# Gate products in blocks of 1024 columns with seven-product quads, placed first, then delta groups, v, u and z

## The chip, the cores and the metric

The kernel runs on one core of a Trainium2 chip. The metric is the device time of one launch in microseconds. The matrix engine is called PE here, the vector engine DVE, the scalar engine ACT, GpSimd POOL, and SP is the queue that issues the loads and stores.

## The reference

One layer, 256 positions, width 4096, all in float32:

```python
def reference(x, norm_g, w_in, ...):
    h = rms_norm(x, norm_g[l])
    proj = h @ w_in[l]                                  # 4096 x 22560
    u_pre, v_pre, z_gm, qkv_pre, z_dn, b_pre, a_pre, gate_gm, gate_dn = split_columns(proj)
    y_gm = gmlp_spatial_gating(gelu(u_pre), gelu(v_pre), ln_g[l], ln_b[l], w_s[l], b_s[l])
    y_gm = (y_gm * silu(z_gm)) @ w_br_gmlp[l]           # 2048 x 4096
    qkv = silu(causal_depthwise_conv(qkv_pre, conv_w[l]))
    q, k, v = ...                                       # 16 heads of 128, q and k normalised
    o = gated_delta_rule(q, k, v, beta, g)              # chunks of 64, a triangular solve in each
    y_dn = (rms_norm(o, dn_norm_g[l]) * silu(z_dn)) @ w_br_dn[l]
    merged = sigmoid(gate_gm) * y_gm + sigmoid(gate_dn) * y_dn
    return rms_norm(x + merged @ w_out[l], final_g)
```

The two gates take 8192 of the columns of w_in.

## The kernel before

A float32 product is made of three fast ones: each operand is split into a rounded part h and a rest l, and xh·h + xh·l + xl·h is summed in PSUM (`mms`, lines 170 to 179; L177 is xh·h, L178 xh·l, L179 xl·h). The sequence's two halves of 128 positions are m = 0 and 1; the split of x stays in SBUF as `xs` (eight tiles, h and l of four row tiles each).

A **job** is 512 columns of a weight matrix: all row tiles (32 of 128 rows for `w_in` and `w_out`, 16 for the two `w_br`), two at a time (`KPD`). A unit of two row tiles is one load of 512 KB (`raw`, five buffers, `fetch`), one cast on ACT (`wh`, L166), one subtraction on DVE (`wl`, L167) and 12 products of 128x512 on PE into two PSUM banks (`acc`, six buffers in pool `pm`; two more banks, `side`, serve all else through `bank()`). `wh` and `wl` have four buffers each. `stream` (L181 on) walks over all units in the order of the list `jobs` and writes the split of a unit three units ahead of its products (`LEAD`).

The order of jobs (L905 on): four v, then u and z by turns (four each), then four delta groups of v, k, q and z_dn (`done_conv`, `done_zd`), each followed by three gate jobs (`done_gate`; the last group by seven), then 16 half jobs of `w_br`, then 8 of `w_out`. After a job its `done` puts a generator in lane 0, which evicts the banks and does the elementwise work; lane 1 holds the longer chains: the delta rule of a group, `dn_gen`, which begins when q's conv is done, and at the end the loads of `ys`. `step` advances both lanes once per unit, a `yield n` waits n units, and `drain` runs them empty (before the pools are closed and opened anew: `open_a`, `open_c`, `open_d`). A scheduler then orders the instructions of each engine; engines work in that order.

A conv (L479 to L534) evicts a job to `vtok`, `ktok` or `tok`, stores it, loads it back shifted by 1 to 3 rows (`tok4`, four buffers) and multiplies and adds on DVE (L501, L503, L504); k and q are turned by a transpose on DVE and 24 corner copies, 12 per half, on ACT (`turn`, L126 to L135). The solve in `dn_gen` is 31 pairs of small operations on DVE (L613, L615).

Of the kernel before, what the change touches and what calls it, by code (L numbers as in the profile page):

```python
# [31 lines left out]
WARM = 9  # L32


class Job:
    def __init__(self, w, col, nk, src, done, before=None):
        self.w, self.col, self.nk, self.src = w, col, nk, src
        self.done, self.before = done, before


@with_exitstack
def trunk(ctx, tc, t):
# [10 lines left out]
    def bank():  # L53
        return ps.tile([P, 512], F32, name="side")
# [125 lines left out]

    def stream():  # L181
        units = [(j, k) for j in jobs for k in range(0, j.nk, KPD)]
        raws, sp, acc, late = {}, {}, None, []
        for i in range(len(units) + LEAD):
            if i == 0:
                for n in range(4):
                    raws[n] = fetch(*units[n], n == 0)
                    first_x(n)
            elif i + 3 < len(units):
                first_x(i + 3)  # L190
                raws[i + 3] = fetch(*units[i + 3])
            if i < len(units):
                if i == 0:
                    sp[i] = split0(raws.pop(i))
                else:
                    split_x(i)
                    sp[i] = split(raws.pop(i), i >= len(units) - TAIL)
            n = i - LEAD
            if n >= 0:
                j, k = units[n]  # L200
                if k == 0:
                    if j.before:
                        j.before()
# [45 lines left out]
    lng = pb.tile([P, W], F32, name="lng")  # L249
    lnb = pb.tile([P, W], F32, name="lnb")  # L250
    wst = pb.tile([P, 16, P], F32, name="wst")
    bs = pb.tile([P, 16], F32, name="bs")
    vg = [pb.tile([P, W], F32, name=f"vg{m}") for m in range(2)]
    vsum = pb.tile([P, 8], F32, name="vsum")
    st = pb.tile([P, 16], F32, name="st")

    def norm_gen():
        yield 12
        xend = xs[KT // 4 - 1][:, 1, 3, S - 1:S].bitcast(F32)
        for m in range(2):  # L260
            for c in range(8):
                xt = pb.tile([P, NC], F32, name="xt", bufs=3)
# [12 lines left out]
    def const_gen():  # L275
        yield 36
        zz = pb.tile([3, NC], F32, name="zz")
        after([lng[:, 0:1], lnb[:, 0:1], wst[:, 0, 0:1], bs[:, 0:1], dng[:, 0:1], alog[:, 0:1], dtb[:, 0:1],
               ident[:, 0:1], upr[:, 0:1], low[:, 0:1], zz[:, 0:1]], rstd[:, 1:2])
        nc.sync.dma_start(out=ident, in_=t["ident"])  # L280
        nc.sync.dma_start(out=lng, in_=t["ln_g"].partition_broadcast(P))
        yield 2
        nc.sync.dma_start(out=lnb, in_=t["ln_b"].partition_broadcast(P))
        yield 2
        nc.sync.dma_start(out=wst, in_=t["w_sT"])
        yield 2
        G.memset(wst[64:P, :, 0:64], 0.0)
        nc.sync.dma_start(out=bs, in_=t["b_sT"])
# [702 lines left out]
```

## Time and profile before

| | |
|---|---|
| median of three runs | 2736.73 us (2734.74 to 2739.87) |
| the profiled execution | 2738.57 us |
| its span | 2736.8 us |
| PE busy | 2708.8 us, 99% |
| DVE busy | 1613.9 us, 59% |
| ACT busy | 1379.4 us, 50% |
| granted clock of PE | 0.998 of full |

The span goes from the first to the last instruction. Busy time is the union of an engine's instructions; a product is 389 ns long in the records but the next starts 0.23 us later, so counts per stretch tell PE's rate better than busy time does.

### The profile page before, as it was taken

What the parts mean: (1) busy time and instruction counts of PE and PEld (TensorE: products, weight loads), DVE (VectorE), ACT (ScalarE), POOL (GpSimd) and SP (SyncE); (2) the same over time, 40 slices, a digit from 0 to 9 for tenths busy, and PEclk for the clock granted to TensorE, in tenths of its full rate; (3) what the DMA queues carried; (4) which work ended last, traced back from release to release, by engine and by line L of the source; (5) the groups of instructions that cost most, each with busy time, mean ns of one, the idle gap of its engine ahead of it and who ended that gap; (6) DMA issues with size and microseconds to landing.
All of it is one profiled execution on the core that took longest, in us unless ns stands there. A gap on an engine that the chain in (4) does not pass through costs nothing.

```text
span 2736.8 us, 33340 instructions
## 1 busy us (share of the span) xinstructions
PE 2708.8 (99%) x12385; PEld 2235.7 (82%) x12385; DVE 1613.9 (59%) x2092; ACT 1379.4 (50%) x1917; POOL 38.2 (1%) x44
## 2 busy tenths in 40 slices
PE   9999999999999999999999999999999999999998
PEld 7888888888788877888788887888878888888886
DVE  6464555466665676746757576564556656645544
ACT  7544555455544455445554456444545655644443
POOL 0000000000000000000000000000000000000000
PEclk9999999999999999999999999999999999999999
DMA  9866676677777676767767676776776666576665
GB/s 327 264 182 202 200 195 197 182 241 241 232 208 200 216 261 202 216 192 232 256 200 211 212 236 218 206 216 177 230 257 210 224 209 223 178 244 217 207 216 170
DMA packets 325292, 595.57 MB, mean 218 GB/s; under 512 B 33636, under 2 KB 47972, under 8 KB 324744
## 3 DMA queue, kind: packets, MB, share of 16 engines
q1 hardware_dynamic: 324840, 593.28, 70.8%
q8 instruction: 97, 1.59, 0.2%
q14 instruction: 67, 0.55, 0.1%
q10 hardware_dynamic: 288, 0.15, 0.0%
HBM read 569.16 MB, written 24.19 MB: 217 GB/s over the span
## 4 chain that ended last, share of the span: by engine, by line
PE 85%; DMA 4%; DVE 4%; ACT 3%; issue 2%; POOL 1%; SPq 0%; DVEq 0%; POOLq 0%
PE acc L177 28%; PE acc L178 28%; PE acc L179 27%; DVE wl L167 1%; DMA cw<-conv_w 1%; ACT wh L166 1%; DMA preq<-tok 1%; ACT kT L135 1%; DVE tok L503 1%; DMA yr<-yds 1%; DMA prek<-ktok 1%; DMA raw<-w_in 0%; DMA yr<-ygs 0%; DMA tok<-prek 0%; POOL rq L97 0%
## 5 line engine op out<-in xcount | busy, mean ns | idle before, releaser
L167 DVE TENSOR_TENSOR wl<-raw,wh 128x1024 fp32r<-128x1024 f32 x954 | 1160.8, 1223 | 928.6 <-ACT wh L166 920.4
L166 ACT CAST wh<-raw 128x1024 fp32r<-128x1024 f32 x954 | 994.9, 1050 | 1196.7 <-PE acc L179 1119.0
L178 PE MATMUL acc<-wl,xs 128*128 128x512 f32 x3308 | 1291.5, 391 | 8.5 <-DVE wl L167 8.1
L177 PE MATMUL acc<-wh,xs 128*128 128x512 f32 x3308 | 1286.9, 391 | 7.3 <-ACT wh L166 7.0
L179 PE MATMUL acc<-wh,xs 128*128 128x512 f32 x3308 | 1285.8, 390 | 0.0
L178 PEld LDWEIGHTS acc<-wl,xs 128*128 128x128 f32 x3308 | 621.8, 188 | 144.4 <-DVE wl L167 17.6
L177 PEld LDWEIGHTS acc<-wh,xs 128*128 128x128 f32 x3308 | 621.2, 188 | 140.0 <-ACT wh L166 10.5
L179 PEld LDWEIGHTS acc<-wh,xs 128*128 128x128 f32 x3308 | 621.4, 188 | 128.6
L179 PE MATMUL acc<-wh,ys 128*128 128x512 f32 x512 | 199.2, 389 | 0.0
L178 PE MATMUL acc<-wl,ys 128*128 128x512 f32 x512 | 199.2, 389 | 0.0
L177 PE MATMUL acc<-wh,ys 128*128 128x512 f32 x512 | 195.8, 389 | 0.0
L179 PEld LDWEIGHTS acc<-wh,ys 128*128 128x128 f32 x512 | 96.1, 188 | 20.1
L178 PEld LDWEIGHTS acc<-wl,ys 128*128 128x128 f32 x512 | 96.1, 188 | 20.0
L177 PEld LDWEIGHTS acc<-wh,ys 128*128 128x128 f32 x512 | 96.1, 188 | 19.8
L503 DVE TENSOR_TENSOR tok<-tok,cw 128x512 f32<-128x512 f32 x72 | 46.5, 688 | 21.9 <-DMA tok<-prek 9.6
L135 ACT COPY sg<-yr 32x128 f32<-32x128 f32 x192 | 56.9, 296 | 2.5
L613 DVE TENSOR_TENSOR tm<-xs,nl 128x248 f32<-128x248 f32 (+30 forms) x124 | 36.2, 292 | 8.7 <-DMA nl<-nscr 5.4
L135 ACT COPY qT<-tmp 32x128 f32<-32x128 f32 x96 | 28.4, 296 | 20.1 <-DVE tmp L126 18.9
L615 DVE TENSOR_TENSOR xs<-xs,tm 128x248 f32<-128x248 f32 (+30 forms) x124 | 36.0, 291 | 3.2
L135 ACT COPY kT<-tmp 32x128 f32<-32x128 f32 x96 | 28.4, 296 | 12.9 <-DVE tmp L126 11.8
L135 ACT COPY zt<-yt 32x128 f32<-32x128 f32 x96 | 28.5, 296 | 1.8 <-DVE yt L126 0.6
L135 ACT COPY big<-tmp 32x128 f32<-32x128 f32 x96 | 28.5, 296 | 1.3
(218 smaller groups left out, 878.8 us busy)
## 6 DMA issues: line engine op xcount, KB each, us to landing
raw<-w_in SPq DMA_DIRECT2D x703, 512.0 KB
raw<-w_out SPq DMA_DIRECT2D x128, 512.0 KB
raw<-w_br_gmlp SPq DMA_DIRECT2D x64, 512.0 KB
raw<-w_br_dn SPq DMA_DIRECT2D x64, 512.0 KB
cw<-conv_w SPq DMA_DIRECT2D x48, 256.0 KB
sg<-sgs SPq DMA_DIRECT2D x16, 512.0 KB
sgs<-tok SPq DMA_DIRECT2D x14, 512.0 KB
tok<-prev SPq DMA_DIRECT2D x12, 512.0 KB
```

The lines of the kernel that those rows point to most:

```text
L135: A.copy(o, i)
L166: A.copy(h, raw)
L167: V.tensor_tensor(out=l, in0=raw, in1=h.bitcast(F32), op=ALU.subtract)
L177: T.matmul(acc[m], lhsT=xh, rhs=h[:, kk], start=f, stop=False)
L178: T.matmul(acc[m], lhsT=xh, rhs=l[:, kk], start=False, stop=False)
L179: T.matmul(acc[m], lhsT=xl, rhs=h[:, kk], start=False, stop=e)
L503: V.tensor_tensor(out=h[:, m], in0=h[:, m], in1=cw, op=ALU.mult)
L613: V.tensor_tensor(out=tv, in0=xs[:, :, j:j + 1].broadcast_to([P, 8, n]), in1=nl[:, j, j + 1:].unsqueeze(1).broadcast_to([P, 8, n]), op=ALU ...
L615: V.tensor_tensor(out=xs[:, :, j + 1:], in0=xs[:, :, j + 1:], in1=tv, op=ALU.subtract)
```

## The change

Two gate jobs stay as they were and come first. Then come six **blocks** of 1024 gate columns (`Block`), each of 16 quads: two row tiles by two column tiles of 512 by the two halves m. With tiles x00..x11 and w00..w11, a quad with an even number is formed from seven products P1 to P7 of sums of x tiles and sums of w tiles; an odd one from the eight plain products. All quads of a block add up in the same eight PSUM banks, six `acc` and both `side` (`block_acc`): P1 to P7, and P8 for the plain quads alone. At the end of a block nine operations (`sums_out`) put the four outputs together in SBUF.

An even quad is four pieces: a (x00 with w01, one tile), b (w12: P6 and P5), d (w34: P7 and P4), c (row tile 1: P2 and P3); an odd one two pieces n0 and n1, one per row tile, of 12 products. `quad_split` makes the sums of w on DVE (`tt`) and the splits. The sums of x are made once (`forms_gen`, `gforms`), beside the second job. Loads are one row tile of 1024 columns, still 512 KB.

Then follow the four delta groups with no gates between, then v, u and z, two plain gate jobs, and the rest as before. Pools are opened by tiles freed (`reuse_waits`), `px` holds what the blocks need, `pa` and `pq` serve the delta groups, `pv` and `pb` the gating. `tok4` has three buffers, `kT` and `qT` two, `big` is shared with the solve's `nl`; a conv of group g waits until group g - 2 is through; `done_v(0)` empties lane 0 and `done_u` empties the lanes up to the load of `lng` and its like.

```diff
+SEVEN = tuple(range(0, 16, 2))
+    def block_acc():
+        acc = {n: pm.tile([P, 512], F32, name="acc") for n in ("P1", "P6", "P7", "P5", "P4", "P2")}
+        acc["P3"], acc["P8"] = bank(), bank()
+        return acc
+    def quad_mms(p, h, l, acc):
...
+        work = {
+            "a": lambda: (("P1", x(0, 0), 0),),
+            "b": lambda: (("P6", form(1), 1), ("P5", form(0), 0)),
+            "d": lambda: (("P7", form(2), 0), ("P4", x(1, 1), 1)),
+            "c": lambda: (("P2", x(0, 1), 1), ("P3", form(3), 0)),
+            "n0": lambda: (("P8", x(1, 0), 0), ("P4", x(1, 0), 1), ("P2", x(0, 0), 1), ("P3", x(0, 0), 0)),
+            "n1": lambda: (("P8", x(1, 1), 0), ("P4", x(1, 1), 1), ("P2", x(0, 1), 1), ("P3", x(0, 1), 0)),
+        }[p.kind]()
...
+    def cut(h, l, src):
+        A.copy(h, src)
+        V.tensor_tensor(out=l, in0=src, in1=h.bitcast(F32), op=ALU.subtract)
+    def quad_split(p, raw):
+        r0, r1 = raw
+        if p.kind == "a":
...
+            V.tensor_tensor(out=t12[:, 0], in0=r0[:, 0], in1=r0[:, 1], op=ALU.add)
+            V.tensor_tensor(out=t12[:, 1], in0=t12[:, 0], in1=r1[:, 0], op=ALU.subtract)
...
+            cut(h, l, r0[:, 1:2])
+            V.tensor_tensor(out=t34[:, 0], in0=r0[:, 1], in1=t12[:, 1], op=ALU.subtract)
+            V.tensor_tensor(out=t34[:, 1], in0=r1[:, 1], in1=t12[:, 1], op=ALU.subtract)
...
+        cut(h, l, {"b": lambda: p.job.tt[p.k][0], "d": lambda: p.job.tt.pop(p.k)[1],
+                   "c": lambda: r1, "n0": lambda: r0, "n1": lambda: r1}[p.kind]())
...
+    def sums(dst, a):
+        V.tensor_tensor(out=dst[:, 0], in0=a[:, 0, 1], in1=a[:, 1, 1], op=ALU.add)
+        V.tensor_tensor(out=dst[:, 2], in0=a[:, 0, 0], in1=a[:, 0, 1], op=ALU.subtract)
+        V.tensor_tensor(out=dst[:, 1], in0=dst[:, 0], in1=a[:, 0, 0], op=ALU.subtract)
+        V.tensor_tensor(out=dst[:, 3], in0=a[:, 1, 0], in1=dst[:, 1], op=ALU.subtract)
+    def forms_gen():
+        yield 15
+        for q in SEVEN:
...
+            V.tensor_tensor(out=a.rearrange("p k m s -> p k (m s)"), in0=x[:, 0, k0:k0 + 2].bitcast(F32),
+                            in1=x[:, 1, k0:k0 + 2].bitcast(F32), op=ALU.add)
+            sums(f, a)
+            cut(gforms[q][:, 0], gforms[q][:, 1], f)
+            yield 2
...
+    def sums_out(acc, p, z):
...
+                ("P1", lambda: A.copy(z1[:, 0], acc["P1"])),
+                ("P6", lambda: V.tensor_tensor(out=z0[:, 0], in0=acc["P6"], in1=z1[:, 0], op=ALU.add)),
+                ("P7", lambda: V.tensor_tensor(out=z1[:, 1], in0=z0[:, 0], in1=acc["P7"], op=ALU.subtract)),
+                ("P5", lambda: V.tensor_tensor(out=z0[:, 0], in0=acc["P5"], in1=z0[:, 0], op=ALU.subtract)),
+                ("P5", lambda: V.tensor_tensor(out=z0[:, 1], in0=acc["P5"], in1=z1[:, 1], op=ALU.subtract)),
+                ("P4", lambda: V.tensor_tensor(out=z1[:, 1], in0=acc["P4"], in1=z1[:, 1], op=ALU.add)),
+                ("P2", lambda: V.tensor_tensor(out=z1[:, 0], in0=acc["P2"], in1=z1[:, 0], op=ALU.add)),
+                ("P3", lambda: V.tensor_tensor(out=z0[:, 0], in0=acc["P3"], in1=z0[:, 0], op=ALU.add)),
+                ("P8", lambda: V.tensor_tensor(out=z0[:, 1], in0=acc["P8"], in1=z0[:, 1], op=ALU.add))):
...
     def tok4():
-        return pa.tile([P, 2, NC], F32, name="tok4", bufs=4)
+        return pq.tile([P, 2, NC], F32, name="tok4", bufs=3)
...
         def f(acc):
             def gen():
+                while dn_done[0] < g - 1:
+                    yield
...
+    for i in (0, 2):
+        jobs.append(Job(win, GG0 + i // 2 * NC, KT, xsrc, done_gate(i)))
+    for i in (1, 4, 5, 8, 9, 12):
+        jobs.append(Block(win, gcol[i % 2] + i // 2 * NC, KT, xsrc, gforms, done_gates(i), need_forms))
+    for g in range(4):
+        jobs.append(Job(win, VV0 + g * NC, KT, xsrc, done_conv("v", g)))
+        jobs.append(Job(win, K0 + g * NC, KT, xsrc, done_conv("k", g)))
+        jobs.append(Job(win, Q0 + g * NC, KT, xsrc, done_conv("q", g)))
+        jobs.append(Job(win, ZD0 + g * NC, KT, xsrc, done_zd(g)))
...
     for c in range(4):
         jobs.append(Job(win, V0 + c * NC, KT, xsrc, done_v(c)))
...
-        for i in range(g * 3, 16 if g == 3 else g * 3 + 3):
...
+    for i in (13, 15):
+        jobs.append(Job(win, GD0 + i // 2 * NC, KT, xsrc, done_gate(i), open_c if i == 13 else None))
```

**The border of two jobs or blocks.** On PE before, where one gate job of 512 columns (acc_5594, acc_5595) gives way to the next (acc_5966, acc_5967):

```order
L179 MATMUL acc_5594<-wh_5872,xs7_95 128x512
L177 MATMUL acc_5595<-wh_5872,xs7_95 128x512
L178 MATMUL acc_5595<-wl_5873,xs7_95 128x512
L179 MATMUL acc_5595<-wh_5872,xs7_95 128x512
L177 MATMUL acc_5966<-wh_5893,xs0_88 128x512
L178 MATMUL acc_5966<-wl_5894,xs0_88 128x512
L179 MATMUL acc_5966<-wh_5893,xs0_88 128x512
L177 MATMUL acc_5967<-wh_5893,xs0_88 128x512
```

On PE now, at the end of the first block (its last quad's piece n1, wh_1650) and the start of the second; acc_1734, acc_1736 and acc_1735 are P6, P5 and P7 of the new block, side_1739 its P3:

```order
L235 MATMUL side_1025<-wl_1651,xs7_95 128x512
L236 MATMUL side_1025<-wh_1650,xs7_95 128x512
L235 MATMUL acc_1734<-wl_1678,gf0_154 128x512
L236 MATMUL acc_1734<-wh_1677,gf0_154 128x512
L235 MATMUL acc_1736<-wl_1678,gf0_154 128x512
L236 MATMUL acc_1736<-wh_1677,gf0_154 128x512
L234 MATMUL acc_1735<-wh_1687,gf0_154 128x512
L235 MATMUL acc_1735<-wl_1688,gf0_154 128x512
L236 MATMUL acc_1735<-wh_1687,gf0_154 128x512
L234 MATMUL side_1739<-wh_1703,gf0_154 128x512
L235 MATMUL side_1739<-wl_1704,gf0_154 128x512
L236 MATMUL side_1739<-wh_1703,gf0_154 128x512
```

Before, a new job has banks of its own; now side_1739 stands in the bank that the old block's P3 had, and its first product waits for DVE.

On DVE before, among the gate jobs of group 0, where no border shows; L669 and L675 belong to the delta chain:

```order
L167 TENSOR_TENSOR wl_6862<-raw_6764,wh_6861 128x1024
L669 STREAM_TRANSPOSE tmp2_6895<-big_6540 64x4x64
L669 STREAM_TRANSPOSE tmp2_6896<-big_6540 64x4x64
L675 COPY tmp2_6895<-tmp2_6895 32x4x32 x2
L675 COPY tmp2_6896<-tmp2_6896 32x4x32 x2
L167 TENSOR_TENSOR wl_6880<-raw_6803,wh_6879 128x1024
```

On DVE now, the same border: L993 to L998 are sums of the old block, L264 to L269 sums of w for a quad of the new one, L256 splits:

```order
L993 TENSOR_TENSOR sg_1030<-acc_1022,sg_1030 128x512
L994 TENSOR_TENSOR sg_1030<-acc_1022,sg_1031 128x512
L264 TENSOR_TENSOR tt_1760<-tt_1760,raw_1656 128x512
L256 TENSOR_TENSOR wl_1688<-tt_1659,wh_1687 128x1024
L268 TENSOR_TENSOR tt_1761<-raw_1654,tt_1760 128x512
L256 TENSOR_TENSOR wl_1704<-raw_1571,wh_1703 128x1024
L269 TENSOR_TENSOR tt_1761<-raw_1656,tt_1760 128x512
L998 TENSOR_TENSOR sg_1030<-side_1026,sg_1030 128x512
L995 TENSOR_TENSOR sg_1031<-acc_1023,sg_1031 128x512
L996 TENSOR_TENSOR sg_1031<-acc_1024,sg_1031 128x512
L997 TENSOR_TENSOR sg_1030<-side_1025,sg_1030 128x512
L256 TENSOR_TENSOR wl_1730<-raw_1631,wh_1729 128x1024
```

The adds that free the banks stand behind the splits and most of the sums of the next quad.

**The solve of a delta group.** On DVE before, in group 1, the solve (L613, L615) with the splits of gate jobs:

```order
L613 TENSOR_TENSOR tm_8750<-xs_8749,nl_8748 128x8x30
L167 TENSOR_TENSOR wl_8711<-raw_8647,wh_8710 128x1024
L615 TENSOR_TENSOR xs_8749<-xs_8749,tm_8750 128x8x30
L613 TENSOR_TENSOR tm_8750<-xs_8749,nl_8748 128x8x29
L615 TENSOR_TENSOR xs_8749<-xs_8749,tm_8750 128x8x29
L613 TENSOR_TENSOR tm_8750<-xs_8749,nl_8748 128x8x28
L167 TENSOR_TENSOR wl_8733<-raw_8668,wh_8732 128x1024
L615 TENSOR_TENSOR xs_8749<-xs_8749,tm_8750 128x8x28
L613 TENSOR_TENSOR tm_8750<-xs_8749,nl_8748 128x8x27
L615 TENSOR_TENSOR xs_8749<-xs_8749,tm_8750 128x8x27
L167 TENSOR_TENSOR wl_8755<-raw_8686,wh_8754 128x1024
```

On DVE now, in group 1 (L822, L824 are the solve; L710 to L713 the conv of k in group 2):

```order
L822 TENSOR_TENSOR tm_7201<-xs_7200,big_7199 128x8x14
L187 TENSOR_TENSOR wl_7367<-raw_7298,wh_7366 128x1024
L824 TENSOR_TENSOR xs_7200<-xs_7200,tm_7201 128x8x14
L712 TENSOR_TENSOR tok4_7408<-tok4_7408,cw_7406 128x512 x2
L822 TENSOR_TENSOR tm_7201<-xs_7200,big_7199 128x8x13
L713 TENSOR_TENSOR ktok_7316<-ktok_7316,tok4_7408 128x512
L187 TENSOR_TENSOR wl_7389<-raw_7319,wh_7388 128x1024
L713 TENSOR_TENSOR ktok_7316<-ktok_7316,tok4_7408 128x512
L824 TENSOR_TENSOR xs_7200<-xs_7200,tm_7201 128x8x13
L187 TENSOR_TENSOR wl_7417<-raw_7340,wh_7416 128x1024
L822 TENSOR_TENSOR tm_7201<-xs_7200,big_7199 128x8x12
L712 TENSOR_TENSOR tok4_7460<-tok4_7460,cw_7458 128x512 x2
```

The conv of the next group now stands among the steps of the solve.

**The end of the delta groups.** On ACT before, the corner copies of q in group 3:

```order
L166 CAST wh_13198<-raw_13128 128x1024
L135 COPY qT_13367<-tmp2_13369 32x4x32 x12
L135 COPY qT_13367<-tmp2_13442 32x4x32 x5
L166 CAST wh_13216<-raw_13152 128x1024
L135 COPY qT_13367<-tmp2_13442 32x4x32 x7
L166 CAST wh_13242<-raw_13170 128x1024
```

On ACT now, around the end of the last delta job, where lane 0 is emptied: the turn of k in group 3, the silu (L715) and squares (L722) of q, the eviction of z_dn (L753):

```order
L715 ACT_TABLE_LOAD
L715 ACTIVATE tok4_11683<-tok4_11683 128x1024
L155 COPY kT_11490<-tmp2_11492 32x4x32 x12
L155 COPY kT_11490<-tmp2_11577 32x4x32 x4
L186 CAST wh_11266<-raw_11194 128x1024
L155 COPY kT_11490<-tmp2_11577 32x4x32 x8
L722 ACTIVATE tmp2_11758<-tok4_11683 128x512
L722 ACTIVATE tmp2_11761<-tok4_11683 128x512
L753 ACTIVATE zg_11282<-acc_10896,rstd_102 128x512
L186 CAST wh_11289<-raw_11214 128x1024
L753 ACTIVATE zg_11282<-acc_10897,rstd_102 128x512
L186 CAST wh_11317<-raw_11236 128x1024
```

What was apart by many casts before, k's turn, q's silu and z_dn's eviction, now stands between three casts.

## Rows read from the trace of the kernel before

**Rows 1.** The page, busy time of each engine (share of the span) and instructions
```profile
PE 2708.8 (99%) x12385; PEld 2235.7 (82%) x12385; DVE 1613.9 (59%) x2092; ACT 1379.4 (50%) x1917; POOL 38.2 (1%) x44
```

**Rows 2.** Busy time by stretches, a delta group with its gates and a stretch of products
```profile
core 0: us, PE busy (x) PEld busy (x) DVE busy (x) ACT busy (x) POOL busy (x), PEclk, DMA share, GB/s
...
1000.00:1305.00 305.00, 301.47 (x1438) 248.21 (x1438) 191.91 (x271) 152.58 (x202) 5.34 (x4) 1.00 0.73 217
...
2200.00:2600.00 400.00, 400.00 (x1767) 331.21 (x1766) 226.88 (x256) 200.89 (x297) 0.00 (x0) 1.00 0.66 214
```

**Rows 3.** Groups of instructions on PE by line and shape, one product line
```profile
line engine op names shapes xcount | busy us, mean ns | idle before us <-releasers
L178 PE MATMUL acc<-wl,xs 128*128 128x512 f32 x3308 | 1291.5, 391 | 8.5 <-DVE wl L167 8.1
...
L178 PE MATMUL acc<-wl,ys 128*128 128x512 f32 x512 | 199.2, 389 | 0.0
...
L178 PE MATMUL acc<-wle,xs 128*128 128x512 f32 x20 | 7.9, 395 | 0.0
```

**Rows 4.** Waits of PE over the whole span: us, times, longest
```profile
engine line waited for: us in total, times, longest us
PE acc L178 <- DVE wl L167: 8.1, 12, 1.4
PE acc L177 <- ACT wh L166: 7.0, 7, 1.5
```

**Rows 5.** Groups by line and shape on DVE and on ACT
```profile
L167 DVE TENSOR_TENSOR wl<-raw,wh 128x1024 fp32r<-128x1024 f32 x954 | 1160.8, 1223 | 928.6 <-ACT wh L166 920.4 <-DMA nl<-nscr 4.5 <-DMA raw<-w_in 1.5
L503 DVE TENSOR_TENSOR tok<-tok,cw 128x512 f32<-128x512 f32 x72 | 46.5, 688 | 21.9 <-DMA tok<-prek 9.6 <-DMA tok<-preq 5.7 <-DMA tok<-prev 4.6
L811 DVE TENSOR_TENSOR sg<-acc,sg 128x512 f32<-128x512 f32 x32 | 20.5, 682 | 0.0
...
L166 ACT CAST wh<-raw 128x1024 fp32r<-128x1024 f32 x954 | 994.9, 1050 | 1196.7 <-PE acc L179 1119.0 <-DMA raw<-w_in 26.6 <-issue 14.5
...
L571 ACT ACT_TABLE_LOAD x8 | 10.3, 1283 | 0.1
```

**Rows 6.** Timeline of DVE (start, us, operation, count), operations in a row
```profile
202.40 2.50 DVE L341 TENSOR_TENSOR vg<-vg,lnb 128x512 f32<-128x512 f32 x4
204.80 3.50 DVE L167 TENSOR_TENSOR wl<-raw,wh 128x1024 fp32r<-128x1024 f32 x3
```

**Rows 7.** The page, loads and stores
```profile
DMA packets 325292, 595.57 MB, mean 218 GB/s; under 512 B 33636, under 2 KB 47972, under 8 KB 324744
```

**Rows 8.** Waits of PE in the four delta groups, 690 to 1980 us
```profile
PE acc L178 <- DVE wl L167: 6.7, 10, 1.4
PE acc L177 <- ACT wh L166: 6.2, 6, 1.5
```

**Rows 9.** Timelines of ACT and of PE at the turn of q in group 1
```profile
1039.42 5.24 ACT L135 COPY qT<-tmp 32x128 f32<-32x128 f32 x17 [4.70 <-DVE tmp L126]
1044.68 1.04 ACT L166 CAST wh<-raw 128x1024 fp32r<-128x1024 f32 x1
1045.75 2.14 ACT L135 COPY qT<-tmp 32x128 f32<-32x128 f32 x7
...
1045.78 0.74 PE L177 MATMUL acc<-wh,xs 128*128 128x512 f32 x2 [1.32 <-ACT wh L166]
```

**Rows 10.** Timeline of PE and the stretches around 2000 us (clock third from the end)
```profile
1999.02 0.49 PE L177 MATMUL acc<-wh,xs 128*128 128x512 f32 x1 [0.87 <-ACT wh L166]
2000.47 0.60 PE L178 MATMUL acc<-wl,xs 128*128 128x512 f32 x1 [0.96 <-DVE wl L167]
...
2000.70:2004.10 3.40, 3.40 (x9) 2.63 (x9) 3.12 (x3) 1.11 (x2) 0.00 (x0) 0.50 0.75 213
2004.10:2010.00 5.90, 5.90 (x27) 4.87 (x27) 2.45 (x2) 2.10 (x2) 0.00 (x0) 1.00 0.91 295
```

More of the change, by code (lines that the diff above doesn't have):

```diff
@@ new lines, in block_acc, with plain, form, x @@
+    def block_acc():
+        acc = {n: pm.tile([P, 512], F32, name="acc") for n in ("P1", "P6", "P7", "P5", "P4", "P2")}
+        acc["P3"], acc["P8"] = bank(), bank()
+        return acc
+    def plain(job, k, m):
+        a, r = job.src(k)
+        return [a[:, i, r, m * P:(m + 1) * P] for i in range(2)]
+    def quad_mms(p, h, l, acc):
+        job, q = p.job, p.k // 2
+        sm = job.forms.get(q)
+        def form(i):
+            return [sm[:, e, i] for e in range(2)]
+        def x(m, kk):
+            return plain(job, p.k + kk, m)
+        work = {
[6 more added lines that the diff above has]
+        }[p.kind]()
+        for name, (xh, xl), i in work:
+            job.left[name] -= 1
+            f, e = name not in job.begun, job.left[name] == 0
+            job.begun.add(name)
+            T.matmul(acc[name], lhsT=xh, rhs=h[:, i], start=f, stop=False)
+            T.matmul(acc[name], lhsT=xh, rhs=l[:, i], start=False, stop=False)
+            T.matmul(acc[name], lhsT=xl, rhs=h[:, i], start=False, stop=e)
@@ L247, in split_xk @@
                                op0=ALU.mult, op1=ALU.subtract)
[L249 to L255, printed above, removed]
+    st = px.tile([P, 16], F32, name="st")
     def norm_gen():
@@ L303, in trunk, with need_forms, open_v @@
+    have_forms = []
+    def need_forms():
+        while not have_forms:
+            step()
     lanes[0].append(norm_gen())
+    lanes[1].append(forms_gen())
     lanes[1].append(const_gen())
+    phb, phv = ExitStack(), ExitStack()
+    pb = pv = None
+    late_ = {}
+    def open_v():
+        nonlocal pv
+        pv = phv.enter_context(tc.tile_pool(name="pv", bufs=1, side="right", reuse_waits="tile"))
+        late_["vg"] = [pv.tile([P, W], F32, name=f"vg{m}") for m in range(2)]
+        late_["vsum"] = pv.tile([P, 8], F32, name="vsum")
@@ L306, in done_v, with need_b @@
+    def need_b():
+        while "open" not in late_:
+            step()
     def done_v(c):
         def f(acc):
+            if c == 0:
+                drain((0,))
+                phq.close()
+                open_v()
+            vg, vsum = late_["vg"], late_["vsum"]
             def gen():
@@ L318, in ln_gen @@
     def ln_gen():
+        while "open" not in late_:
+            yield
+        vg, vsum, lng, lnb = (late_[n] for n in ("vg", "vsum", "lng", "lnb"))
         mu = pb.tile([P, 2], F32, name="mu")
@@ L347, in f @@
         def f(acc):
+            need_b()
             u = pb.tile([P, 2, NC], F32, name="gu", bufs=2)
@@ L761, in f @@
             z = (pc.tile([P, 2, NC], F32, name="sg", bufs=4) if pc else
-                 tok4())
+                 pb.tile([P, 2, NC], F32, name="gu", bufs=2) if pb else px.tile([P, 2, NC], F32, name="sg", bufs=3))
             def gen():
@@ L770, in done_gate, with done_gates, f, gen @@
         return f
+    def sums_out(acc, p, z):
+        job = p.job
+        z0, z1 = z
+        for need, do in (
+                ("P1", lambda: A.copy(z1[:, 0], acc["P1"])),
[7 more added lines that the diff above has]
+                ("P8", lambda: V.tensor_tensor(out=z0[:, 1], in0=acc["P8"], in1=z0[:, 1], op=ALU.add))):
+            while job.left[need]:
+                yield
+            do()
+    def done_gates(i0):
+        def f(acc, p):
+            job = p.job
+            if p.first:
+                job.z = [px.tile([P, 2, NC], F32, name="sg", bufs=3) for _ in range(2)]
+                job.out = sums_out(acc, p, job.z)
+            if next(job.out, "end") == "end":
+                def gen():
+                    for c in range(2):
+                        for m in range(2):
+                            A.activation(job.z[c][:, m], job.z[c][:, m], AF.Sigmoid, scale=rstd[:, m:m + 1])
+                        yield
+                        nc.sync.dma_start(out=sgs[i0 + 2 * c], in_=job.z[c])
+                lanes[0].append(gen())
+        return f
     phc = ExitStack()
```

263 lines of the change are left out of this document (176 added, 87 removed).

## The prediction

> **What bounds the kernel now.** I read the page's busy times first: PE is busy 99% of the span, DVE 59%, ACT 50% [rows 1]. Busy PE is not yet PE at its peak, so next the stretch table: between 2200 and 2600 us, where hardly anything but products runs, PE starts 1767 instructions in 400 us, one per 226.4 ns, at a granted clock of 1.00 [rows 2]. The groups of one product line give 3308 + 512 + 20 = 3840 products [rows 3]; with three lines that makes 11,520, and 11,520 x 0.2264 = 2608 us of 2736.8. The rest is small products, the warm-up and the last stores. The waits of PE are 8.1 + 7.0 us in the whole run [rows 4]. So only fewer products make this kernel shorter, as long as DVE and ACT still deliver their operands in time. They deliver ahead of PE: DVE idles 928.6 us ahead of its splits, nearly all of it because it waits for a cast on ACT [rows 5], and the casts wait for PE to give back one of four buffers.
>
> **What the change removes.** Six blocks of 1024 gate columns have 16 quads (two row tiles by two column tiles by two halves of the sequence). A plain quad takes 8 tile products of 3 instructions, 24 in all; a quad of the new form takes 7, so 21. Eight quads per block save 6 x 8 x 3 = 144 instructions: 144 x 0.2264 = **32.6 us**. The order shows exactly that, 11,376 against 11,520 long products. Nothing else leaves PE.
>
> **What it adds on DVE, inside the blocks.** A quad of the old form costs DVE two subtractions of 128x1024. Three of these in a row fill 3.50 us and one takes 1.22, so each further one costs (3.50 - 1.22) / 2 = 1.14 us; four 128x512 operations fill 2.50 us, so (2.50 - 0.69) / 3 = 0.60 each [rows 6]. A quad of the new form costs five small and three large ones, 3.0 + 3.42 = 6.4 us, while PE needs 21 x 0.2264 = 4.75 us for it: alone, DVE would be the bound. But every second quad is plain: DVE 2.28, PE 5.43. For the pair DVE has 8.7 us of work in PE's 10.2, about 1.5 us to spare. DVE's work for one new quad can be done while PE is in the plain one, since four operand buffers hold about one quad. I cost the inside of the blocks at nothing; the cover is those 1.5 us per pair. ACT has 5 casts of 1.05 and one half as long, 5.8 of 10.2 us [rows 5]. DMA must bring 2.1 MB per 10.2 us, 206 GB/s, against a mean of 218 over the kernel before [rows 7]: nothing.
>
> The rows show that the next DVE operation starts before the recorded end of the last: 0.60 apart [rows 6], 0.69 long [rows 5]. A rule of the Trainium skill ("VectorE: DVE Perf Modes", section Terms) says otherwise and speaks against this change: a pipeline flush follows every DVE operation, and the next can't issue until the pipe is empty. Charged by whole recorded durations, a pair would cost 5 x 0.69 + 5 x 1.22 = 9.6 us, plus 0.7 for its share of the block's sums: 10.3, more than PE's 10.2. I take the spacing of the rows; the other is a rival.
>
> **What it adds at the border of two blocks.** All eight PSUM banks belong to a block. Nine sums bring the seven products together, one copy on ACT and eight adds of 128x512 from PSUM on DVE; such an add (out of PSUM) took 0.68 us [rows 5], 0.60 in a row. The order shows where they stand: four of them behind the splits of the next block's first quad, and PE's P3 products, 8 after the old block's end, wait for the last. From PE's start on the second piece of the last new quad I count DVE's queue: it first waits 0.9 us for P6, then has eight adds for the sums (4.8), five large subtractions (5.7) and five small operations of the next quads (3.0), 13.5 us, so it is done at 14.4. PE has 57 products to do before it needs that bank, 12.9 us. It waits 1.5 us. In two of the five borders between blocks (after the second and the fifth) two of the small operations stand behind the sums, which leaves 0.3. 3 x 1.5 + 2 x 0.3 = **5.1 us** (0 if DVE is ahead by another 1.5; 15 if each border costs 3).
>
> **The way into the first block.** Eight sets of sums of x, 2.5 us of DVE each (two 512s, four 128s at 0.3), are made beside the second job, where DVE has 16 x (2.72 - 1.14) = 25 us free for these 20. They also delay the first block's own sums: **1 us** (0 to 4).
>
> **The moved work.** The four delta groups lose the three gate jobs (more in the last) that stood behind each. Before, a group of seven jobs had 191.9 us of DVE work in 305 [rows 2], of which 112 splits at about 1.17 are 131; the other 61 now stand in four jobs: 64 x 1.17 + 61 = 136 in some 182 us, 75%. Throughput is there. What grows is waiting in order: the order shows the conv of the next group's v, k and q among the 32-step solve of this one, so a conv operation that waits for its load holds up the solve and the splits behind it. DVE waited 21.9 us in all for conv loads [rows 5], and PE's waits in the four groups were 6.7 + 6.2 = 12.9 us [rows 8]. I take half as much again, **6 us**; the bounds are -6 (half of the old waits go) and 32 (8 more per group, rival 4). SP's queue carries the same conv loads at a denser spacing, with three tok4 buffers for four; ahead of the splits the raw tiles wait in five buffers, which is the cover.
>
> At two points the lanes are emptied (first v job, first u job), and ACT has more between two casts than PE takes to use them up: at the first v job a table load of 1.28, a silu of about 1, 24 corner copies of 0.31, three activations of about 0.6 and two casts, 13 us in PE's 5.4. With four buffers ACT can be three pieces less a cast ahead, 3 x 2.72 - 1.05, about 7 us. The nearest row is a burst of 5.2 us, one cast and 2.1 more, after which PE waited 1.3 [rows 9]. **2.5 us** for both (0 to 8). The changed order of PSUM banks costs nothing: the v job of the fourth group is emptied late, but still 48 products before its bank is needed.
>
> **Sum.** -32.6 + 5.1 + 1 + 6 + 2.5 = -18.0. The profiled execution has a span of 2736.8 and took 2738.57 us, 1.8 around the span; the median of the runs is 2736.73, so the span stands for the median and I forecast 2736.7 - 18.0 = **2719 us**.
>
> **Rivals.** (1) Nearly all of the gain arrives: DVE is ahead at the borders and the delta groups wait no more than before: -32.6 + 3 gives 2707. For it: the waits before are few [rows 4]. Against: the queue count at the borders.
> (2) DVE bounds the blocks, by full durations: 8 x 9.6 + 8 x 0.69 = 82 us per block against PE's 81.5, and no slack to make up a wait: some 2 us at each of six blocks on top of 3 for the rate, so -32.6 + 3 + 12 + 9.5 (the terms outside the blocks) gives 2729. Against: the spacing [rows 6].
> (3) The clock falls at the borders. After two waits of 0.87 and 0.96 us within 1.5 us the granted clock stood at 0.50, the 1.2 GHz level, from 2000.7 to 2004.1 [rows 10], which loses 1.7 us. Five of these: 2719 + 8.5 = 2728. Against: waits of up to 1.5 us in the delta groups [rows 8] left the clock at 1.00 [rows 2]. The Trainium skill, "TensorE: Matmul & The Clock Gate", section What's actually happening, says that the throttled state is the default and that activity lifts it; the row of 0.50 agrees.
> (4) Slower: the delta groups. Conv loads and the solve hold each other up in DVE's queue, and the small products in PE's. It decides from 24 us on (32.6 less 8.6 for the other terms), 6 per group on top of the 3.2 of now; at 8 it is 2736.7 - 32.6 + 8.6 + 32 = 2745. Against: DVE at 75%, and waits of 3 us in a group where DVE was at 63%.
> That the products don't become fewer is ruled out by the order.
>
> **How the numbers follow.** Forecast (2712 to 2728) 0.48; rival 1 0.15; rival 2 0.12; rival 3 0.08; rival 4 0.12; half of rival 4 (2731 to 2742) 0.05. About 0.2% (5.5 us) can be told from no change, so faster is below 2731.3: 0.48 + 0.15 + nearly all of 2 and 3, 0.78. Same: the rest of these, half of rival 4 and its near edge, 0.12. Slower 0.10. The range 2705 to 2741 leaves out the best end of rival 1 and most of rival 4.
>
> **What will show it.** 11,376 long products at 226 ns. Within a block, no wait of PE for DVE or ACT longer than 0.3 us; at five borders one wait for a DVE add, 0.4 to 1.6 us; DVE at about 90% in the blocks. Spacing of DVE's 512s at 0.69 would show rival 2, a PEclk under 1.00 in the first third rival 3. PE's waits in the delta groups should be 15 to 25 us; above 35 I'm wrong. At the start of the v jobs PE should wait 1 to 2 us for a cast.

## The result, and the profile after

The changed kernel took **2752.0 us** (median of five runs, 2747.6 to 2753.1) against 2736.7 (2734.7 to 2739.9) before: a ratio of 1.0051 (1.0036 to 1.0065), so it is slower by 0.5%. The forecast was 2719, in a range of 2705 to 2741. The profiled execution has a span of 2751.3 us, 14.5 more than before.

The page's busy times, to be laid beside [rows 1]:

```profile
PE 2697.4 (98%) x12241; PEld 2208.1 (80%) x12241; DVE 1843.7 (67%) x2476; ACT 1453.0 (53%) x2023; POOL 40.1 (1%) x40
```

PE has 12,385 - 12,241 = 144 instructions fewer, as forecast, but its busy time fell by only 11.4 us. The waits tell where to look. First those of all engines from 85 to 575 us, a stretch within the six blocks (which end at 625 us here), then those of PE alone there, those of SP's queue (which issues the loads), and those of PE in the delta groups (575 to 1400 us) and behind them (1700 to 1725 us):

```profile
engine line waited for: us in total, times, longest us
ACT s L255 <- DMA raw<-w_in: 120.1, 38, 6.9
...
DVE tt L263 <- DMA raw<-w_in: 51.8, 33, 5.6
```
```profile
PE side L234 <- DVE sg L998: 8.9, 5, 1.9
PE acc L235 <- DVE wl L256: 5.3, 11, 0.9
PE acc L234 <- ACT wh L255: 2.9, 2, 2.4
PE acc L234 <- ACT s L255: 2.1, 4, 0.7
PE side L235 <- DVE wl L256: 2.1, 4, 0.8
```
```profile
SPq L311 <- DVE wl L256: 247.1, 128, 7.0
SPq L311 <- DVE tt L268: 144.8, 43, 8.5
```
```profile
PE acc L198 <- DVE wl L187: 8.3, 13, 2.1
PE acc L197 <- ACT wh L186: 5.0, 6, 1.5
```
```profile
PE side L576 <- DVE vg L543: 4.6, 1, 4.6
```

L255's cast `s<-raw` and L263's sum `tt<-raw` are the first steps of an **a piece**, the piece of a seven-product quad that forms the sums. ACT and DVE stand there for a load, 38 and 33 times; there are 48 a pieces in the six blocks. The loads themselves are issued late, since SP waits 144.8 us for L268, a sum of an a piece, to free a raw tile. In the delta groups PE waits 8.3 + 5.0 us, about what [rows 8] showed (6.7 + 6.2). Behind them is one wait that the kernel before did not have, for the layer norm of v (L543).

The chain of waits in the first block (start, us, what; lines left out at ...) shows a loop:

```profile
87.72 5.19 DMA raw<-w_in
...
92.93 0.69 DVE tt L263
93.62 1.13 DVE wl L256
94.76 0.60 DVE tt L264
...
95.88 0.69 DVE tt L268
...
97.08 1.23 DVE wl L256
98.31 0.02 issue
98.33 5.39 DMA raw<-w_in
...
103.75 0.69 DVE tt L263
...
111.42 6.41 DMA raw<-w_in
...
122.11 4.53 DMA raw<-w_in
...
133.72 4.39 DMA raw<-w_in
...
145.80 6.58 DMA raw<-w_in
```

A load lands and the a piece starts (92.93); behind its sums comes the first of three splits (97.08), which frees the tile for the load that the next a piece needs (98.33), and that lands 5.4 us later (103.72). From load to load the five turns up to 145.80 take 58.1 us, 11.6 each, where PE's products for a pair of quads should take 10.2, and no work of PE stands in this part of the chain. Of the whole chain from 85 to 575 us, 33% are such loads.

The same stretch by engine: PE starts 1988 instructions.

```profile
core 0: us, PE busy (x) PEld busy (x) DVE busy (x) ACT busy (x) POOL busy (x), PEclk, DMA share, GB/s
85.00:575.00 490.00, 468.50 (x1988) 370.50 (x1987) 416.56 (x488) 263.08 (x292) 0.00 (x0) 1.00 0.63 201
```

### The profile page after: what moved, and what is told of

Read it like the earlier page. It is cut to its first block, busy times and chain, and to the rows that moved or that the text cites. A ratio compares the mean times of both kernels' runs of the same rounds, so it can differ in the third digit from the quotient of the medians.

```text
span 2751.3 us, 33611 instructions
## 1 busy us (share of the span) xinstructions
PE 2697.4 (98%) x12241; PEld 2208.1 (80%) x12241; DVE 1843.7 (67%) x2476; ACT 1453.0 (53%) x2023; POOL 40.1 (1%) x40
## 4 chain that ended last, share of the span: by engine, by line
PE 67%; DVE 12%; DMA 12%; issue 4%; ACT 3%; SPq 1%; POOL 0%; DVEq 0%; POOLq 0%; ACTq 0%
PE acc L198 20%; PE acc L197 20%; PE acc L199 20%; DMA raw<-w_in 6%; DVE wl L256 3%; DVE wl L187 2%; PE acc L235 1%; PE acc L236 1%; PE acc L234 1%; DMA tok<-preq 1%; ACT wh L186 1%; DMA preq<-tok 1%; DVE tok L712 1%; DVE tt L264 1%; PE side L235 1%
## 5 line engine op out<-in xcount | busy, mean ns | idle before, releaser
L187 DVE TENSOR_TENSOR wl<-raw,wh 128x1024 fp32r<-128x1024 f32 x762 | 925.8, 1221 | 655.3 <-ACT wh L186 652.0
L186 ACT CAST wh<-raw 128x1024 fp32r<-128x1024 f32 x762 | 794.9, 1052 | 893.5 <-PE acc L199 822.0
L198 PE MATMUL acc<-wl,xs 128*128 128x512 f32 x2540 | 993.7, 391 | 9.3 <-DVE wl L187 9.1
L199 PE MATMUL acc<-wh,xs 128*128 128x512 f32 x2540 | 990.4, 390 | 0.0
L197 PE MATMUL acc<-wh,xs 128*128 128x512 f32 x2540 | 984.5, 392 | 5.7 <-ACT wh L186 5.3
L198 PEld LDWEIGHTS acc<-wl,xs 128*128 128x128 f32 x2540 | 478.0, 188 | 115.4 <-DVE wl L187 17.8
L197 PEld LDWEIGHTS acc<-wh,xs 128*128 128x128 f32 x2540 | 477.2, 188 | 108.1 <-ACT wh L186 8.7
L199 PEld LDWEIGHTS acc<-wh,xs 128*128 128x128 f32 x2540 | 477.7, 188 | 98.9
L255 ACT CAST wh<-raw 128x1024 fp32r<-128x1024 f32 x144 | 149.4, 1050 | 92.3 <-PE side L236 77.3
L256 DVE TENSOR_TENSOR wl<-raw,wh 128x1024 fp32r<-128x1024 f32 x144 | 172.3, 1220 | 10.1 <-ACT wh L255 9.8
L235 PE MATMUL acc<-wl,xs 128*128 128x512 f32 x288 | 114.2, 396 | 4.1 <-DVE wl L256 4.0
L256 DVE TENSOR_TENSOR wl<-tt,wh 128x1024 fp32r<-128x1024 f32 x96 | 116.3, 1219 | 1.9 <-ACT wh L255 1.8
L236 PE MATMUL acc<-wh,xs 128*128 128x512 f32 x288 | 112.8, 392 | 0.0
L255 ACT CAST wh<-tt 128x1024 fp32r<-128x1024 f32 x96 | 99.3, 1047 | 21.6 <-PE acc L236 12.1
L234 PE MATMUL acc<-wh,xs 128*128 128x512 f32 x288 | 97.4, 392 | 0.0
L255 ACT CAST s<-raw 128x512 fp32r<-128x512 f32 x48 | 29.8, 621 | 125.0 <-DMA raw<-w_in 125.0
```

What stands on the lines that cost most here:

```text
L186: A.copy(h, raw)
L187: V.tensor_tensor(out=l, in0=raw, in1=h.bitcast(F32), op=ALU.subtract)
L197: T.matmul(acc[m], lhsT=xh, rhs=h[:, kk], start=f, stop=False)
L198: T.matmul(acc[m], lhsT=xh, rhs=l[:, kk], start=False, stop=False)
L199: T.matmul(acc[m], lhsT=xl, rhs=h[:, kk], start=False, stop=e)
L234: T.matmul(acc[name], lhsT=xh, rhs=h[:, i], start=f, stop=False)
```

## Experiments

All ratios below are to the kernel before, measured beside it. "Lost in the blocks" is worked out from the row of 85 to 575 us: in a kernel that loses nothing there (e9, below), PE starts 2133 instructions, one per 0.2297 us; each one missing is that much lost. For the changed kernel that is 145 x 0.2297 = **33.3 us**, about what the 144 products should have saved. (From the first product of the blocks to the last it is the same: 530.3 us in the changed kernel, 497.1 in e9.)

The first theory (A) was that the raw tiles come free too late. Its rivals: DVE's own work (B), the sums at the borders (C), the new order of the stages (D).

### Nine raw tiles (e1)

```
-        room = {"wp": 5, "x": 1}
+        room = {"wp": 5, "x": 4}
-            get(n + (4 if p.kind == "std" else 5))
+            get(n + (4 if p.kind == "std" else 8))
```

The second raw pool has four tiles, and the gate results have two instead of three.

> The blocks hold nine raw tiles instead of six (three more in the second pool; to make the room no more than the bank for gate results goes from three to two tiles). Theory A, late loads: in the blocks the loads are issued in bursts of four, each burst only when the sum of the a piece has freed a raw tile, and take 3.1 to 6.2 us to land, so that ScalarE and VectorE stand in their order behind an a piece whose tile has not come (125 us of ScalarE's waits). With three more tiles these waits fall below 40 us, the first block's seven waits of PE (7 us) go, and of the 39 us that PE loses from 85 to 570 us some 20 come back: 2728 to 2735 us. Rival B, VectorE itself bounds the blocks (its recorded 0.69 us and 1.22 us an operation): nothing changes, 2749 to 2753 us. Rival C, the borders: the first block's 7 us come back, the five borders (16 to 20 us) stay, 2743 to 2747 us.

Measured: 2729.1 us, 0.9969 (0.9956 to 0.9981); 2098 instructions in the blocks, 8.0 us lost. The time is as A expected, and B and C fall: DVE has the same operations, the borders the same sums, and PE doesn't wait for one of them. But ACT's waits for loads at the a piece are still 66.9 us (A expected under 40), and SP still waits 124.6 us for L268.

### Plain blocks (e2)

```
-SEVEN = tuple(range(0, 16, 2))
+SEVEN = ()
```

The nine sums at a block's end become four copies, and a `yield 16` stands for the waits of the eight sets of forms that are no longer made.

> The blocks stay, 1024 columns wide and in the same place, but all their quads are of the plain form: 144 products more (32.6 us) and no a, b, c, d pieces, no sums on VectorE but four copies at a block's end. Theory A: two loads are freed evenly per 24 products, so PE loses in the blocks little more than the kernel before did, about 8 us instead of 39, and the time is 2751 + 32.6 - 31 = 2753 us. Rival C, the borders cost what they do through the handing over of the two side banks, which the plain form keeps: about 20 us lost in the blocks, 2764 us. Rival D, the new order of the stages behind the blocks costs the gain: nothing of the 39 us is there, and the time beyond 570 us is as in the changed kernel in either case.

Measured: 2753.2 us, 1.0054 (1.0039 to 1.0070), as by A. PE doesn't wait once in the blocks, borders included. (Some 8 us are lost ahead of them, in the two plain jobs: 294 instructions from 10 to 85 us against 330.) So the blocks' shape, their eight banks and the new order of the stages don't cost the 33 us; something that comes with the seven-product quads does, the a pieces or the nine sums at the borders.

### The order u0, u1, z0, z1 (e3), and with nine tiles (e4)

```
-    for c in range(4):
-        jobs.append(Job(win, U0 + c * NC, KT, xsrc, done_u(c)))
-        jobs.append(Job(win, ZG0 + c * NC, KT, xsrc, done_z(c)))
+    for c in (0, 2):
+        for i in range(2): ... done_u(c + i)
+        for i in range(2): ... done_z(c + i)
```

> The u and z products of two column groups change places: u0, u1, z0, z1 instead of u0, z0, u1, z1, so that the layer norm of v has one more job (43 us) before the spatial product of z0 asks for it. If the wait of 4.77 us at 1711 us and the 6.83 us at the lower clock behind it come from the burst of the layer norm right ahead of that product, both go and 7 to 8 us come back: 2744 us. If the burst is only moved and the next product waits for it instead, the time stays at 2752 us.

> Both edits, the nine raw tiles and the order u0, u1, z0, z1. The two losses lie 1100 us apart and share no queue, so the gains add: by theory A 2720 to 2728 us, by rival C 2735 to 2740 us, by rival B 2744 us.

Measured: e3 2749.1, 1.0037 (1.0024 to 1.0049); PE's wait for the layer norm is still there, 4.2 us at 1707 us. e4 2730.2, 0.9967 (0.9955 to 0.9980), no less than e1 alone. So the gains that both expected did not come: a job more ahead of the product doesn't help, since the layer norm doesn't wait for its turn among the jobs. In the program it waits for the room of the last delta group (`open`); in the changed kernel the gate functions of u0 and z0 and the layer norm start together at 1697.7 to 1700.3 us, behind the 24 copies of that group on ACT.

### Eight, seven and five raw tiles (e5, e6, e7)

The same edit with other numbers (room and lead of the loads); the gate results keep their three tiles.

> Eight raw tiles in the blocks and nothing else changed (the three gate tiles stay, so the two tiles of the nine-tile kernel are not what helped). Theory A (raw tiles come free late): nearly all of what nine tiles gave, PE loses 7 to 12 us from 85 to 575 us where it lost 33, and the time is 2729 to 2735 us. Rival: the smaller bank of gate results or the other order that nine tiles led to made the gain; then the time stays near 2750 us.

> Seven raw tiles, nothing else changed. Theory A: a part of the gain, PE loses 12 to 22 us from 85 to 575 us, 2735 to 2742 us. If a single tile already breaks the bursts of four loads, it is all of it, 2730 us.

> Five raw tiles, one less than the changed kernel. Theory A: an a piece's loads are issued one split later; a pair of quads (10.2 us of products, 48 pairs) takes 1 to 3 us more, 2800 to 2890 us. Rival B (VectorE is the bound) or C (the borders): within 10 us of 2752.

| raw tiles | time, us | lost in the blocks, us | a casts that stand ahead of b or d casts of earlier quads (of 48) |
|---|---|---|---|
| 5 (e7) | 2731.0, one run | 9.9 | 1 |
| 6 (changed kernel) | 2752.0 | 33.3 | 33 |
| 7 (e6) | 2752.6, ratio 1.0051 (1.0036 to 1.0067) | 36.3 | 47 |
| 8 (e5) | 2735.4, ratio 0.9989 (0.9981 to 0.9998) | 20.2 | 47 |
| 9 (e1) | 2729.1 | 8.0 | 47 |

The losses are read from one profiled execution each, in e6 and e5 one that took some 5 and 4 us more than the median. Theory A as it stood falls: it expected 2800 us and more with five tiles, 2735 to 2742 with seven and a loss of 7 to 12 us with eight. One tile less helps about as much as three more (e7 is a single run), and a seventh does nothing. In e7 ACT even waits longer for loads than in the changed kernel, yet PE loses little (waits in the blocks):

```profile
ACT s L255 <- DMA raw<-w_in: 126.1, 44, 5.6
```

What five tiles changed is the order. The kernel's scheduler sets the order of each engine's instructions, and it gave another one with another number of tiles. The last column counts it on ACT. In the changed kernel a piece's cast (s2_1317, reading the next quad's raw_1224) stands ahead of the b and d casts of the quad before (from tt_1228 and tt_1229), in e9 behind them:

```
changed kernel, ACT                       e9, ACT
CAST s2_1317<-raw_1224 128x512            CAST wh_1244<-tt_1228 128x1024
CAST wh_1244<-tt_1228 128x1024            CAST wh_1254<-tt_1229 128x1024
CAST wh_1254<-tt_1229 128x1024            CAST s2_1317<-raw_1224 128x512
CAST wh_1270<-raw_1138 128x1024           CAST wh_1270<-raw_1138 128x1024
```

New theory (E): the place decides. An a piece that stands too far ahead holds up, while its load is on the way, the very splits that PE needs next (b and d) and those that free the tiles for the next loads (c and the plain quad's). The table also shows what E leaves out: at the same count, 47 of 48, seven, eight and nine tiles lose 36.3, 20.2 and 8.0 us. Where the place is wrong, more tiles do help.

### The a piece behind b and d, six tiles (e9)

```
+        if p.kind == AFTER:                   # "d": its cast and its subtraction
+            behind[:] = two
...
+            if p.kind == "a":
+                for i in behind:
+                    es.enter_context(tc.issue_after(i))
```

This sets the order of issue of the a piece on ACT and on DVE and adds no wait; the scheduler places the rest anew around it.

> Six raw tiles as in the changed kernel, but on ScalarE and VectorE every a piece is queued behind the splits of the b and d pieces of the seven-product quad before it (in the changed kernel it stands ahead of them, two splits of 1.05 and 1.13 us each further to the front). Five tiles gave 2731 us and seven 2753 us, so the number of tiles alone is not the cause. Theory E, the place: with five tiles, too, the a piece stands behind b and d; if the place decides, PE loses under 10 us from 85 to 575 us where it lost 33, and the time is 2726 to 2732 us. Theory A, the tiles: order alone gives back under 8 us, 2744 to 2752 us.

Measured: **2721.1 us**, 0.9933 (0.9919 to 0.9946), 31 less than the changed kernel with the same tiles, loads, banks and operations, and 5 less than E expected. The stretch of the blocks, and ACT's and SP's waits there (the edit moves the lines: L256 is L255, L325 is L311, L280 is L268):

```profile
85.00:575.00 490.00, 490.00 (x2133) 400.06 (x2132) 447.62 (x521) 286.87 (x312) 0.00 (x0) 1.00 0.64 215
```
```profile
ACT s L256 <- DMA raw<-w_in: 31.6, 20, 3.4
```
```profile
SPq L325 <- DVE wl L258: 367.9, 138, 7.9
...
SPq L325 <- DVE tt L280: 11.1, 39, 0.9
```

PE is busy all 490 us. Loads wait for splits and hardly for an a piece's sum (11.1 us instead of 144.8). That wait alone says little: it is 124.6 us in e1 and 101.4 in e10 (below), which lose 8.0 and 6.2 us. That the loop is gone shows in the chain of the same stretch, which has only PE's products in it, no load and no split:

```profile
by line: PE acc L235 22.0%; PE acc L237 21.9%; PE acc L236 21.9%; PE side L236 10.7%; PE side L235 10.7%; PE side L237 10.7%; PE acc L200 0.7%; PE acc L199 0.7%; PE acc L198 0.7%
```

So the order is what costs the 33 us. How much of it is the a piece's own place isn't shown apart, since the adds at the borders moved as well (see the borders below).

### Further behind (e10), and nine tiles with this order (e11)

e10 puts the a piece behind all splits of the pair before. e11 is e9's order with nine tiles and with e8's edit (next).

> Six raw tiles, every a piece queued still later, behind all splits of the pair of quads before it. Theory E: an a piece can stand too late as well, since the b and d splits right behind it need its sums; its loads have landed by then, so the waits for loads fall under 40 us on ScalarE, but PE waits for the b splits; the time is between 2730 and 2745 us. If waiting for loads is all that matters, 2725 to 2730 us.

> Nine raw tiles, the a piece behind b and d, and the first half of the layer norm early. Theory E: nine tiles in this place lose no more in the blocks than five or six (under 10 us), so 2723 to 2728 us, the shortest of all; if tiles and place add up, 2718 to 2722 us.

Measured: e10 2725.0, 0.9950 (0.9936 to 0.9963), 6.2 us lost in the blocks: no wait for a load at the a piece is left in the list, but b's cast now waits for the sums right ahead of it (127.4 us of ACT's waits). e11 2721.4, 0.9935 (0.9923 to 0.9948), nothing lost in the blocks. With the place right, tiles add nothing in the blocks. e10's time is not in E's range (2730 to 2745) but at the lower end of the other (waiting for loads is all that matters, 2725 to 2730): an a piece that stands too late costs less than E expected. That it costs something, PE's 6.2 us lost with no load waited for show.

### The layer norm of v (e8, e12)

In e8 the small tiles of the layer norm's first half (mean, squares, root) lie in v's pool, so that this half need not wait for the delta group's room; e8 has nine raw tiles too. e12 has e9's order and six tiles, e8's early first half, and scales each column group just ahead of its own product, behind the newest split:

```
+                yield from scale_v(c)          # in done_z(c), ahead of its product
+            with tc.issue_after(newest[0]):    # in scale_v
```

> Nine raw tiles, and the first half of the layer norm of v (mean, squares, root) no longer waits for the room that the last delta group gives back: its small tiles lie in the pool of v. Only the scaling by the two loaded vectors still waits. In the changed kernel the first half took 11 us (1698 to 1709 us) ahead of the scaling, and PE stood from 1710.9 to 1715.6 us and then ran 6.8 us at the lower clock. If the length of this chain is the cause, the wait falls under 1 us and 7 to 8 us come back against the nine-tile kernel: 2721 to 2723 us. If the scaling itself, two operations of VectorE a tile for eight tiles in front of the product, is what it waits for, it stays at 2729 us.

> The order of e9 (six raw tiles, a behind b and d), and the layer norm of v taken apart: mean, squares and root right after the v products, and the scaling of a column group (four operations of VectorE) only ahead of its own spatial product and behind the newest split. In e9 PE waits 4.83 us at 1678 us for eight scalings by the first vector and the adds behind them, and runs 6.83 us at the lower clock after it, 8.3 us in all. If the burst of sixteen operations of VectorE in one place is the cause, the wait falls under 1 us, the lower clock there goes, and the time is 2721 - 8 = 2713 us (2711 to 2716). If PE waits then for something else of the same backlog (ScalarE's 24 copies of the last delta group, then the gate functions of u0 and z0), it stays at 2718 to 2722 us.

Measured: e8 2727.0, 0.9961 (0.9948 to 0.9974), 2 us below e1 and within its spread. The wait of the product went, and another came in its place: PE waited 3.1 us for a split that stood behind eight scalings in a row. e12: **2715.9 us**, 0.9921 (0.9908 to 0.9935), the shortest of all, 5.2 below e9 (the spreads of the two touch: 2714.7 to 2720.0 and 2718.7 to 2723.3); from 1655 to 1700 us PE's longest wait is 0.7, and the clock there is 1.00 (0.92 in e9). The expectation was 2713 (to 2716).

## Why the prediction was wrong

**The step that failed** is the inside of the blocks, in its cover and in its DMA line: "DVE's work for one new quad can be done while PE is in the plain one", and "DMA must bring 2.1 MB per 10.2 us, 206 GB/s, against a mean of 218 over the kernel before [rows 7]: nothing." Both compare rates, and the rates hold: in e9 every operation of the changed kernel is done in time at 215 GB/s with DVE busy 447.6 of 490 us. What they leave out is that ACT, DVE and SP take their instructions in order and that a load can start only when a tile is free. The step should have asked of the new piece: which load does it wait for, which instruction frees that load's tile, and what stands behind it meanwhile. I had read the order for the number of operations and for the place of the borders' sums, not for the place of the a pieces. The blocks lost 33.3 us, borders and way in included, for which I had 6.1: 27.2 of the miss of 33. Of the 33.3, 8.9 are PE's waits at the borders and 1.7 the lower clock after one of them; the other 22.7 lie inside the blocks, where I had nothing.

**The borders** (5.1 us) were mis-sized in the changed kernel. PE waited at all five, 1.64 to 1.93 us each and 8.9 in all, as forecast for an add on DVE that stands behind splits and sums of the next quad. The first border, on DVE and (last two lines) on PE:

```profile
186.22 0.68 DVE L994 TENSOR_TENSOR sg<-acc,sg 128x512 f32<-128x512 f32 x1
186.82 0.68 DVE L264 TENSOR_TENSOR tt<-tt,raw 128x512 f32<-128x512 f32 x1
187.42 1.22 DVE L256 TENSOR_TENSOR wl<-tt,wh 128x1024 fp32r<-128x1024 f32 x1
188.55 0.69 DVE L268 TENSOR_TENSOR tt<-raw,tt 128x512 f32<-128x512 f32 x1
189.16 1.22 DVE L256 TENSOR_TENSOR wl<-raw,wh 128x1024 fp32r<-128x1024 f32 x1
190.29 0.69 DVE L269 TENSOR_TENSOR tt<-raw,tt 128x512 f32<-128x512 f32 x1
190.89 0.69 DVE L998 TENSOR_TENSOR sg<-side,sg 128x512 f32<-128x512 f32 x1
...
192.69 0.68 DVE L997 TENSOR_TENSOR sg<-side,sg 128x512 f32<-128x512 f32 x1
```
```profile
186.38 0.40 PE L236 MATMUL side<-wh,xs 128*128 128x512 f32 x1
...
191.73 0.77 PE L234 MATMUL side<-wh,gf 128*128 128x512 f32 x1 [1.93 <-DVE sg L998]
```

The add is not the one I had. L998 is that of P8, whose last product is the one at 186.38; L997, that of P3, comes behind PE's start. So the new block's P3 stands in the old P8's bank (not in P3's, as the order above was read), and of the eight adds five are in the queue up to L998, itself among them. By my own prices that is 12.6 us against PE's 12.9 and no wait. DVE came to it later than I counted, and whether by its standing for loads earlier or otherwise was not tried: in e9, where PE doesn't wait there, the same add stands earlier in the order, behind one split, and starts 0.8 us after P8's last product instead of 4.1:

```profile
177.43 1.22 DVE L258 TENSOR_TENSOR wl<-raw,wh 128x1024 fp32r<-128x1024 f32 x1
178.57 0.68 DVE L1012 TENSOR_TENSOR sg<-side,sg 128x512 f32<-128x512 f32 x1
```

The way into the first block (1 us) cost little: from 10 to 85 us PE starts 330 instructions in the changed kernel and 328 in e9, against 331 before.

**The products** were right in number and wrong in price. I took 226.4 ns from a stretch of plain products [rows 2]. Two rows of 200 to 560 us, of e2 (plain quads) and e9, where PE never waits:

```profile
200.00:560.00 360.00, 360.00 (x1590) 298.08 (x1589) 171.70 (x150) 148.57 (x149) 0.00 (x0) 1.00 0.71 208
```
```profile
200.00:560.00 360.00, 360.00 (x1566) 293.82 (x1565) 329.62 (x381) 212.63 (x230) 0.00 (x0) 1.00 0.65 216
```

360/1590 is 226.4 ns, 360/1566 is 229.9: 3.5 ns more, over 6 x 8 x 45 = 2160 products 7.6 us. The seven-product form saves 25 us, not 32.6.

**The delta groups** (6 us): PE's waits are 13.3 us there against 12.9 (the first drain's among them), below my 15 to 25; only a stretch of 3.4 us at the lower clock after a wait of 2.1 us at 1139.8 us is new (1.7 us lost). That is 2.1 for a term of 6. Rival 4, my only way to a slower kernel, did not happen. Slower it became by another one.

**The two drains** (2.5 us): the first is right, PE waits 1.3 us for a cast at the first v job. The second isn't a cast. The layer norm comes in one burst, PE waits 4.6 us for it, until 1715.9 us, and runs at a granted clock of 0.50, the 1.2 GHz level:

```profile
1714.07:1720.90 6.83, 5.04 (x16) 4.39 (x17) 6.83 (x10) 0.46 (x1) 0.00 (x0) 0.50 0.36 94
```

That is 4.6 + (1720.9 - 1715.9)/2 = 7.1 us, where the forecast had 2.5 for both drains; e12 got 5.2 back, by the medians.

**The rivals.** Rival 2 (DVE by whole recorded durations) falls with e9, where nothing is lost in the blocks with the same DVE operations. Two splits in a row there take 2.35 us from start to end with 1.22 recorded for one, so 1.13 apart:

```profile
98.75 2.35 DVE L258 TENSOR_TENSOR wl<-raw,wh 128x1024 fp32r<-128x1024 f32 x2
```

The Trainium skill ("VectorE: DVE Perf Modes", section Terms) has the next operation wait until the pipe is empty; by the trace it starts 0.09 us before the recorded end, and the measurement decides. Rival 3, the clock at the borders, happened once in the changed kernel, 3.41 us at 191.7 us, and not at the other four. It is not out for good: in e6 and e5 the granted clock fell to 0.50 three times each in the blocks, for 13.7 and 10.2 us in all, about 6.8 and 5.1 of their losses in the table.

**The sum, again.** With the order repaired the kernel takes 2721.1, near the 2719 forecast, but not by the forecast's terms, so the nearness is luck: the price of the products (+7.6) and the layer norm (+4.6) are made up for by the borders, which cost nothing there (-5.1), and by smaller ones. Among these are the delta groups: in e9 PE waits 12.9 us there, as before, and the granted clock is at 0.50 twice for 3.4 us, 3.4 us lost where I had 6. For the changed kernel the blocks (+27.2), the products (+7.6), the layer norm (+4.6), the delta groups (-3.9) and the ys loads, which I had left out (-2.4: PE waits 1.1 us there, where [rows 10] had 0.87 + 0.96 and 3.4 us at 0.50), make 27.2 + 7.6 + 4.6 - 3.9 - 2.4 = 33.1, the miss.

## What to carry to other kernels

When a change puts a new step in the queues that run in order, follow one turn of it: the load it waits for, the instruction that frees this load's buffer, and what stands behind the step. If the last two meet, the rates of the engines say nothing. And when a scheduler sets the order, change the buffers one at a time in both directions before believing that buffers are short: here one fewer helped about as much as three more, and pinning the order did better than either. The Trainium skill ("DMA: Bandwidth & Descriptors", section Rules for kernel authors) asks to issue a load early and wait for it late; the trace agrees, with loads that took 5.2 and 5.4 us in the chain above, but early is decided by the place of the split that frees the tile.

## What the runs showed of the hardware

- Products in the blocks of seven-product quads start 229.9 ns apart, in plain blocks at the same place 226.4, with PE never waiting in either. It is no sum of a few long gaps: in e9 all starts from 200 to 560 us are 224 to 240 ns apart. Why was not tried.
- A long wait on ACT says little by itself: 126 us for loads in e7, with 9.9 us lost on PE.
- In the changed kernel the granted clock fell to 0.50 right as PE's wait of 1.93 us ended at 191.7 us, and stayed at 1.00 after one of 2.44 us that ended at 526.8 us. What parts the two these rows don't tell.
